# A two-layer hybrid decoder trunk: attention products in split precision, the compressed branch moved to the end of a unit, and the adaLN vectors moved into the FFN blocks

## The chip, the cores and the metric

The kernel runs on one core of one Trainium2 chip. The metric is the device time of the program in microseconds (us), lower is better. All tensors are float32. A product of two float32 tiles is either made directly (F32) or, after a tile has been split into a rounded part (hi, type F32R) and the rest (lo), as three F32R products hi·hi + hi·lo + lo·hi (`mm3`, lines 121 to 124, where the three have a line each).

## The reference

One sequence of 512 positions, width 1024, two layers. Each layer has three sub-layers, each of them modulated by a vector c through shift, scale and gate (adaLN) and closed by a layer norm:

```python
for l in range(DEPTH):
    mod = (silu(c) @ ada_w[l] + ada_b[l]).reshape(Bn, 3, 3, D)   # shift, scale, gate
    x = LN(ALPHA*x + 0.5*(1+gate0) * swiglu(x*(1+scale0)+shift0))
    x = LN(ALPHA*x +     (1+gate1) * mixer (x*(1+scale1)+shift1))
    x = LN(ALPHA*x + 0.5*(1+gate2) * swiglu(x*(1+scale2)+shift2))
```

The mixer is one projection whose columns go to attention, to a gated MLP and to a state-space part, and one output projection over all three. The attention has 8 heads in 2 groups and, for each block of 128 queries, three branches, each with a softmax of its own, weighted with gates and added: compressed keys (31 of them), selected key blocks (all of them here, since the 16 best of 8 are taken), and a window of 512.

## The kernel before

**Order of the work.** Six sub-layers follow each other: FFN, mixer, FFN, FFN, mixer, FFN (n = 0 to 5). An FFN walks over its 22 column blocks in two halves of 11: up products into PSUM, the activation, then the down products. Weights come as 512 KB tiles by DMA from the SP queue, are split by ACT (`hi`) and DVE (`lo`, line 106), and go into `mm3`.

**adaLN vectors.** A vector of 1024 is made by 8 steps of `ada_dot` (line 155): a 512 KB tile of weights is loaded, and DVE multiplies and sums it along its rows with the vector silu(c). `make_bg` hands these steps out: `bg()` is called at fixed places of a sub-layer and issues the next few. The table `share` says how many vectors a sub-layer makes: 4, 3, 3, 3, 3 for n = 0 to 4. Both mixers (n = 1 and n = 4) make three each, beside the attention; `silu_c()` makes silu(c) anew there.

**Attention.** A unit is a pass p (heads 0, 1 or 2, 3 of both groups), a query block qb (3, 2, 1, 0 in this order) and a branch br. There are 24 units in a mixer. `score` makes the scores of four heads (tile S), the softmax numerators (tile P: DVE adds bias and takes the maximum, ACT takes the exponential), and scales them with gate over sum (line 920 on DVE). Two units later `gather` takes the unit in chunks of 128 keys: four transposes on PE (line 938, F32) into a bank of PSUM (`tp`, two banks), a copy to SBUF by ACT (`pt`, line 940), and the product with the values, here called the weigh (line 948): two F32 products, each of which fills one half of the output's partitions (64 value columns) and takes 256 columns of pt. A mixer has 40 chunks in the branches 1 and 2 and 8 in the compressed branch; the two mixers have 80 and 16. All chunks of the three branches of a (p, qb) add up in `op`; after the last, ACT and DVE take it out of PSUM into `hT_hi` and `hT_lo` (lines 958, 959). `op` is a half of the one bank of pool P, so two query blocks share a bank.

**Filler.** Between transposes and weigh, `tick` lets PE go on with a list of jobs: the remaining projections (`pj`), then the part of the output projection that needs no attention (`part`, tile y, closed by `residual`, line 242), and in the second pass `rest`, the part that does. The order of the instructions on every engine is fixed when the program is built, by a scheduler that takes the instruction that it holds to be ready first; on the chip every engine takes them in that order.

Of the kernel before, what the change touches and what calls it, by code (L numbers as in the profile page):

```python
# [11 lines left out]
F32 = mybir.dt.float32  # L12
F32R = mybir.dt.float32r
# [6 lines left out]
T = 512  # L20
# [25 lines left out]
QORDER = (3, 2, 1, 0)  # L46
# [6 lines left out]
def kernel(ctx: ExitStack, tc: tile.TileContext, a: dict, out: bass.AP,  # L53
                             subs=((0, 0), (0, 1), (0, 2), (1, 0), (1, 1), (1, 2))):
    nc = tc.nc
    V, S, G, PE = nc.vector, nc.scalar, nc.gpsimd, nc.tensor
# [14 lines left out]
    def nm(s):  # L71
        count[0] += 1
        return f"{s}_{count[0]}"

    def slab(s, pool="s", dt=F32):
        return sp[pool].tile([128, 512], dt, tag=pool, name=nm(s))

    def big(s):
        return bp.tile([128, 1024], F32, tag="b", name=nm(s))

    def tiny(s, n, dt=F32):
        rot = s in ("mx", "sm", "fc", "st", "mv", "rs", "nr", "gst", "ss")
        return (t4 if rot else t1).tile([128, n], dt, tag=f"t_{s}", name=nm(s))

    def bank(k, s):
        return psp[k].tile([128, 512], F32, tag=k, name=nm(s))
# [34 lines left out]
    def mm3(o, lh, ll, rh, rl, first, last):  # L121
        PE.matmul(o, lh, rh, start=first, stop=False)  # L122
        PE.matmul(o, lh, rl, start=False, stop=False)  # L123
        PE.matmul(o, ll, rh, start=False, stop=last)  # L124
# [17 lines left out]
    def silu_c():  # L142
        csil, c_th = big("csil"), big("cth")
        load(csil, bcast_row(a["c"][0], 1024))
        S.activation(c_th, csil, AF.Tanh, scale=0.5)
        V.scalar_tensor_tensor(csil, c_th, 1.0, csil, op0=ALU.add, op1=ALU.mult)
        cond["c"] = csil
# [43 lines left out]
    def gate_par(l, s, P):  # L191
        g = P["G"] = big("G")
        G.dma_start(g, bcast_row(mods[l, s, 2][0], 1024))
        if s != 1:
            V.tensor_scalar(g, g, 0.25, None, op0=ALU.mult)

    def norm_par(l, s, P):
        P["lg"], P["lb"] = big("lg"), big("lb")
        load(P["lg"], bcast_row(a["ln_g"][l, s], 1024))
        load(P["lb"], bcast_row(a["ln_b"][l, s], 1024))  # L200
# [249 lines left out]
    def mixer(l, P, last, lane, bg, catch_up, gate_params, norm_params):  # L450
# [10 lines left out]
        w2v = p2[:, 256:384]  # L461
        pe = p2[:, 384:416]
        dtb, alog = p2[:, 446:450], p2[:, 450:454]
        dsk, ng = p2[:, 454:456], p2[:, 456:458]
        w3v = wsT.rearrange("p (g t) -> p g t", g=4)
        G.affine_select(w3v, w3v, pattern=[[0, 4], [1, 128]], compare_op=ALU.is_ge, fill=0.0, base=0,
                        channel_multiplier=-1)
# [94 lines left out]
        def pair(t):  # L562
            return [t[:, 0:512], t[:, 512:1024]]
# [250 lines left out]
        V.tensor_sub(kc4[:, :, 1, :], ks4, kc4[:, :, 0, :].bitcast(F32))  # L814
        S.copy(vcm[0:31, :], ps[0:31, 64:192])

        o0 = pair(big("o0"))
        ready = []

# [14 lines left out]
        early = []  # L834
# [93 lines left out]
        def release(n=0):  # L928
            while len(held) > n:
                held.pop(0)()  # L930

        def gather(p, qb, br, pr, op):
            nv = 8 * qb + 7
            for kb in range(1 if br == 0 else qb + 1):
                n = nv if br == 0 else 128
                tp = bank("H", "tp")
                for e in range(4):
                    PE.transpose(tp[0:n, e * 128:(e + 1) * 128], pr[e][:, kb * 128:kb * 128 + n], ident)  # L938
                pt = slab("pt", "q")
                S.copy(pt[0:n, :], tp[0:n, :])  # L940

                def weigh(kb=kb, n=n, pt=pt):
                    for g, r in ((0, lo_half), (1, hi_half)):
                        if br == 0:
                            v = vcm[0:n, g * 64:(g + 1) * 64]
                        else:
                            v = (vS, vW)[br - 1][:, kb * 128 + g * 64:kb * 128 + (g + 1) * 64]
                        PE.matmul(op[r, :], v, pt[0:n, g * 256:(g + 1) * 256], start=(br == 0),  # L948
                                  stop=(br == 2 and kb == qb))
                    if br == 2 and kb == qb:  # L950
                        o3 = op.rearrange("p (i t) -> p i t", i=2)
                        if not ready:
                            early.append(qb)
                            for i in range(2):
                                S.copy(o0[i][:, qb * 128:(qb + 1) * 128], o3[:, i, :])
                            return
                        hh = hT_hi[:, qb, 2 * p:2 * p + 2, :]
                        S.copy(hh, o3)
                        V.tensor_sub(hT_lo[:, qb, 2 * p:2 * p + 2, :], o3, hh.bitcast(F32))

                held.append(weigh)
                tick(TICK_G[p])
                release(HOLD)

        units = [(p, qb, br) for p in range(2) for qb in QORDER for br in range(3)]
        later = {}
        for n, (p, qb, br) in enumerate(units):
            if br == 2 and p == 1:
                later[n + 1] = qb
        def gains(tiles):  # L970
            for k in tiles:
# [50 lines left out]
                    jobs.pop(0)  # L1022
            credit[0] = min(credit[0], 1)

        silu_c()
        probs = [score(*u, TICK_0) for u in units[:LOOK]]
        for n, (p, qb, br) in enumerate(units + [(2, 0, 0)]):
            if n + LOOK < len(units):
                probs.append(score(*units[n + LOOK], TICK_S[n // 12]))
            if n < len(units):  # L1030
                if br == 0:
                    if n % 6 == 0:
                        opt = bank("P", "op")
                    op = opt[:, (n % 6) // 3 * 256:(n % 6) // 3 * 256 + 256]
                gather(p, qb, br, probs[n], op)
            else:
                release()
            bg()
            if n in later:
                jobs.append(rest(later[n]))  # L1040
# [46 lines left out]
    for n, (l, s) in enumerate(subs):  # L1087
        order.append((l, s, 2))
        if n + 1 < len(subs):
            order += [(*subs[n + 1], 1), (*subs[n + 1], 0)]  # L1090
    share = {0: 4, 1: 3, 2: 3, 3: 3, 4: 3}

    def need(*key):
        if key not in mods:
# [49 lines left out]
    for n, (l, s) in enumerate(subs):  # L1144
        last = n == len(subs) - 1
        catch_up = partial(renew, P)
        P = {}

        def params():
            if n:  # L1150
                norm_par(l, s, P)
            if (l, s, 2) in mods:
                gate_par(l, s, P)
            if not last and (*subs[n + 1], 0) in mods:
                next_par(l, s, *subs[n + 1], P)

        if s == 1:
            if not lane:
                for _ in make_bias():
                    pass  # L1160
            need(l, s, 2)
            cond.clear()
            mixer(l, P, last, lane, make_bg(n, P), catch_up, lambda: gate_par(l, s, P), lambda: norm_par(l, s, P))
        else:
            if share.get(n) and "c" not in cond:
                silu_c()
            after_mixer = n > 0 and subs[n - 1][1] == 1
            gated = [None]
            ffn(l, s, P, last, make_bg(n, P, gated), (2, 0) if after_mixer and QORDER[0] == 3 else (0, 2), params,
                catch_up, feed if n == 0 else None, gated)  # L1170
# [90 lines left out]
```

## Time and profile before

| | us |
|---|---|
| median of 3 runs | 2063.02 (2061.39 to 2063.42) |
| the profiled execution, its own time | 2062.94 |
| its span, first to last instruction | 2061.2 |
| PE busy | 2032.4 |
| DVE busy | 1328.4 |
| ACT busy | 764.5 |

The granted clock of PE is full throughout (9 in every slice of the page). A busy PE means that some product is in flight; products overlap, so how fast PE advances is read from the distance between the starts of successive rows of the timeline.

### The profile page before, as it was taken

Reading aid. Unit: us, or ns where it says so; the run is one execution under the profiler, and the core shown is the slowest. Engines: PE = TensorE matmul, PEld = TensorE weight load, DVE = VectorE, ACT = ScalarE, POOL = GpSimd, SP = SyncE. Lnnn points to the kernel's source line nnn. Section 1 sums busy time; section 2 is a strip of 40 time slices with the busy share of each in tenths; the row PEclk is TensorE's granted clock in tenths of the full one; section 3 lists DMA queues with packets and bytes.
Section 4 is the critical chain, followed back from the end, with each engine's and each line's share of the span. In section 5 each row is a group of like instructions: output and inputs, shape, how many; then the busy total and the mean of one; then the engine's idle time right before and its main releaser. Section 6 shows DMA issues by size and latency. Waiting matters only on the chain.

```text
span 2061.2 us, 25919 instructions
## 1 busy us (share of the span) xinstructions
PE 2032.4 (99%) x9992; PEld 1648.3 (80%) x9992; DVE 1328.4 (64%) x2425; ACT 764.5 (37%) x1342; POOL 43.0 (2%) x73
## 2 busy tenths in 40 slices
PE   7999999999999999999999999999999999999998
PEld 6888888987666888888898888889776678888886
DVE  6756438878897647444764644478788975353455
ACT  4422223525657422222442222235256573222221
POOL 0000000000000000000000000000000000000000
PEclk9999999999999999999999999999999999999999
DMA  8755425324452544442444444243254523233221
GB/s 338 259 175 212 153 97 181 106 84 162 138 168 73 193 134 161 135 126 83 161 143 135 151 144 126 88 145 102 92 174 132 169 97 107 79 115 100 93 91 52
DMA packets 85175, 282.34 MB, mean 137 GB/s; under 512 B 13843, under 2 KB 14099, under 8 KB 85052
## 3 DMA queue, kind: packets, MB, share of 16 engines
q1 hardware_dynamic: 82748, 274.88, 40.6%
q0 software_dynamic: 2304, 5.82, 0.8%
q8 instruction: 78, 1.28, 0.3%
q14 instruction: 45, 0.37, 0.1%
HBM read 278.51 MB, written 4.76 MB: 137 GB/s over the span
## 4 chain that ended last, share of the span: by engine, by line
PE 93%; DVE 4%; ACT 1%; DMA 1%; issue 0%; POOL 0%; SPq 0%; DVEq 0%; POOLq 0%; ACTq 0%
PE h L122 15%; PE h L123 15%; PE h L124 15%; PE y L122 9%; PE y L124 9%; PE y L123 9%; PE pj L122 3%; PE pj L124 3%; PE pj L123 3%; PE op L948 2%; PE tp L938 2%; PE S L907 1%; PE S L908 1%; DVE raw L155 1%; PE hps L218 1%; PE hid L641 1%
## 5 line engine op out<-in xcount | busy, mean ns | idle before, releaser
L104 ACT CAST whi<-raw 128x1024 fp32r<-128x1024 f32 x308 | 320.4, 1047 | 747.3 <-issue 393.7
L122 PE MATMUL h<-hT_hi,whi 128*128 128x512 f32 (+1 forms) x1504 | 565.8, 377 | 12.8 <-ACT hT_hi L1081 12.8
L123 PE MATMUL h<-hT_lo,whi 128*128 128x512 f32 (+1 forms) x1504 | 566.4, 377 | 0.0
L124 PE MATMUL h<-hT_hi,wlo 128*128 128x512 f32 (+1 forms) x1504 | 566.1, 376 | 0.0
L106 DVE TENSOR_TENSOR wlo<-raw,whi 128x1024 fp32r<-128x1024 f32 x308 | 372.8, 1216 | 262.0 <-ACT whi L104 261.5
L122 PEld LDWEIGHTS h<-hT_hi,whi 128*128 128x128 f32 x1504 | 283.7, 189 | 63.8 <-ACT hT_hi L1081 12.8
L124 PEld LDWEIGHTS h<-hT_hi,wlo 128*128 128x128 f32 x1504 | 283.9, 189 | 51.5
L123 PEld LDWEIGHTS h<-hT_lo,whi 128*128 128x128 f32 x1504 | 283.9, 189 | 51.5 <-DVE hT_lo L1082 0.4
L124 PE MATMUL y<-whi,glo 128*128 128x512 f32 x576 | 224.2, 389 | 0.0
L122 PE MATMUL y<-whi,ghi 128*128 128x512 f32 x576 | 224.2, 389 | 0.0
L123 PE MATMUL y<-wlo,ghi 128*128 128x512 f32 x576 | 224.2, 389 | 0.0
L333 DVE TENSOR_TENSOR th<-th,h 128x512 f32<-128x512 f32 x88 | 60.4, 687 | 228.6 <-PE h L124 227.9
L155 DVE CUSTOM_DVE_ANT_0 raw<-raw,csil 128x1024 f32<-128x1024 f32 x144 | 174.3, 1218 | 1.6 <-DMA raw<-in_ada_w_dram 1.5
L123 PEld LDWEIGHTS y<-wlo,ghi 128*128 128x128 f32 x576 | 108.2, 188 | 22.5
L124 PEld LDWEIGHTS y<-whi,glo 128*128 128x128 f32 x576 | 108.2, 188 | 22.5
L122 PEld LDWEIGHTS y<-whi,ghi 128*128 128x128 f32 x576 | 108.2, 188 | 22.3
L122 PE MATMUL pj<-hT_hi,whi 128*128 128x512 f32 x288 | 117.4, 408 | 0.0
L123 PE MATMUL pj<-hT_lo,whi 128*128 128x512 f32 x288 | 113.7, 395 | 0.0
L124 PE MATMUL pj<-hT_hi,wlo 128*128 128x512 f32 x288 | 113.4, 394 | 0.0
L102 DVE TENSOR_TENSOR raw<-raw,G 128x1024 f32<-128x1024 f32 x86 | 104.2, 1217 | 2.0 <-DMA raw<-in_w_dram 1.9
L336 ACT CAST ghi<-th 128x512 fp32r<-128x512 f32 x88 | 54.4, 619 | 136.5 <-DVE th L333 136.5
L332 DVE SCALAR_TENSOR_TENSOR th<-th,h 128x512 f32<-128x512 f32 x88 | 60.0, 682 | 38.1 <-ACT th L331 38.1
(285 smaller groups left out, 2516.7 us busy)
## 6 DMA issues: line engine op xcount, KB each, us to landing
raw<-in_w_dram SPq DMA_DIRECT2D x256, 512.0 KB, 3.6
raw<-in_ada_w_dram SPq DMA_DIRECT2D x144, 512.0 KB, 4.4
raw<-in_wS_dram SPq DMA_DIRECT2D x36, 512.0 KB, 3.5
raw<-in_cw_dram SPq DMA_DIRECT2D x16, 512.0 KB, 3.9
raw<-in_wo_dram SPq DMA_DIRECT2D x16, 512.0 KB, 4.5
raw<-in_wl_dram SPq DMA_DIRECT2D x8, 512.0 KB, 9.0
T<-lane SPq DMA_DIRECT2D x16, 256.0 KB, 4.1
lg<-in_ln_g_dram SPq DMA_DIRECT2D x6, 512.0 KB, 5.1
```

The costliest lines, as they stand in the source:

```text
L102: V.tensor_mul(raw, raw, gain)
L104: S.copy(hi[:, :n], raw[:, :n])
L106: V.tensor_sub(lo[:, :n], raw[:, :n], hi[:, :n].bitcast(F32))
L122: PE.matmul(o, lh, rh, start=first, stop=False)
L123: PE.matmul(o, lh, rl, start=False, stop=False)
L124: PE.matmul(o, ll, rh, start=False, stop=last)
L155: V.tensor_tensor_reduce(out=raw, in0=raw, in1=cond["c"], scale=0.5, scalar=0.0, op0=ALU.mult, op1=ALU.add, accum_out=acc[:, k:k + 1])
L332: V.scalar_tensor_tensor(th, th, 1.0, h1, op0=ALU.add, op1=ALU.mult)
L333: freed[0] = V.tensor_mul(th, th, h3).ins
L336: S.copy(hi, th)
L938: PE.transpose(tp[0:n, e * 128:(e + 1) * 128], pr[e][:, kb * 128:kb * 128 + n], ident)
L948: PE.matmul(op[r, :], v, pt[0:n, g * 256:(g + 1) * 256], start=(br == 0), stop=(br == 2 and kb == qb))
```

## The change

The weigh of the branches 1 and 2 becomes an `mm3`: the probabilities are split by ACT (`pt`, now F32R) and DVE (`pl`, a new slab from pool T), the values once for each mixer (`v_hi`, `v_lo`), and each product takes all 128 value columns and all 512 columns of the probabilities. Of its result only the two blocks on the diagonal (a group's values with its own heads) are used. `op` is therefore a whole bank, one for each (p, qb), from a pool that still has one bank. The branches of a (p, qb) come in the order 1, 2, 0, and `settle_heads`, after branch 0, takes each block out of PSUM by itself. The vectors are made in the FFNs alone (`share` 6, 5, 5 for n = 0, 2, 3).

```diff
+        v_hi, v_lo = [pair(bp.tile([128, 1024], F32R, tag="b", name=nm(s_))) for s_ in ("vh", "vl")]
+        for v, h, lo in zip((vS, vW), v_hi, v_lo):
+            S.copy(h, v)
+            V.tensor_sub(lo, v, h.bitcast(F32))
...
+        def settle_heads(p, qb, op):
+            for g, r in ((0, lo_half), (1, hi_half)):
+                o3 = op[r, g * 256:(g + 1) * 256].rearrange("p (i t) -> p i t", i=2)
+                if not ready:
+                    for i in range(2):
+                        S.copy(o0[i][r, qb * 128:(qb + 1) * 128], o3[:, i, :])
+                else:
+                    hh = hT_hi[r, qb, 2 * p:2 * p + 2, :]
+                    S.copy(hh, o3)
+                    V.tensor_sub(hT_lo[r, qb, 2 * p:2 * p + 2, :], o3, hh.bitcast(F32))
...
-                pt = slab("pt", "q")
+                pt = slab("pt", "q", F32 if br == 0 else F32R)
                 S.copy(pt[0:n, :], tp[0:n, :])
-                def weigh(kb=kb, n=n, pt=pt):
+                if br:
+                    pl = slab("pl", "T", F32R)
+                    V.tensor_sub(pl, tp, pt.bitcast(F32))
+                def weigh(kb=kb, n=n, pt=pt, pl=pl if br else None):
+                    if br:
+                        v = slice(kb * 128, (kb + 1) * 128)
+                        mm3(op, v_hi[br - 1][:, v], v_lo[br - 1][:, v], pt, pl, br == 1 and kb == 0, False)
+                        return
                     for g, r in ((0, lo_half), (1, hi_half)):
-                        if br == 0:
-                            v = vcm[0:n, g * 64:(g + 1) * 64]
-                        else:
-                            v = (vS, vW)[br - 1][:, kb * 128 + g * 64:kb * 128 + (g + 1) * 64]
-                        PE.matmul(op[r, :], v, pt[0:n, g * 256:(g + 1) * 256], start=(br == 0),
-                                  stop=(br == 2 and kb == qb))
+                        c = slice(g * 256, (g + 1) * 256)
+                        PE.matmul(op[r, c], vcm[0:n, g * 64:(g + 1) * 64], pt[0:n, c], start=False, stop=True)
+                    settle_heads(p, qb, op)
...
-        units = [(p, qb, br) for p in range(2) for qb in QORDER for br in range(3)]
+        units = [(p, qb, br) for p in range(2) for qb in QORDER for br in (1, 2, 0)]
...
-        silu_c()
...
-                if br == 0:
-                    if n % 6 == 0:
-                        opt = bank("P", "op")
-                    op = opt[:, (n % 6) // 3 * 256:(n % 6) // 3 * 256 + 256]
+                if br == 1:
+                    op = bank("P", "op")
...
-    share = {0: 4, 1: 3, 2: 3, 3: 3, 4: 3}
+    share = {0: 6, 2: 5, 3: 5}
```

Two smaller edits go with it: four columns of a parameter tile are copied to a tile of their own, so that its slab of pool T comes free early (four of its five slabs hold the bias of the pass, tile T, and `pl` takes the fifth), and `next_par` of a mixer moves to where `norm_par` is called.

How the instructions stand: four places in the first mixer. Names carry a buffer's number at the end.

**PE, first query block (qb = 3) of the second pass.** `tp` are transposes, `op` the weighs, `S` scores, `y` filler. Before:

```order
L124 MATMUL y_5102<-whi_4597,hT_lo 128x512
L907 MATMUL S_5154<-kh_3549,qa_4452 128x384
L908 MATMUL S_5154<-kl_3552,qa_4452 128x384
L907 MATMUL S_5160<-kh_3549,qa_4565 128x384
L908 MATMUL S_5160<-kl_3552,qa_4565 128x384
L948 MATMUL op_5055<-pt_5100,vS_2843 64x256 x2
L938 MATMUL tp_5128<-cst,P_4930 128x128
L948 MATMUL op_5055<-pt_5116,vS_2843 64x256 x2
L938 MATMUL tp_5128<-cst,P_4936 128x128
L938 MATMUL tp_5128<-cst,P_4942 128x128
L938 MATMUL tp_5128<-cst,P_4948 128x128
```

With the change:

```order
L122 MATMUL op_5149<-pt_5155,vh_3944 128x512
L123 MATMUL op_5149<-pl_5157,vh_3944 128x512
L124 MATMUL op_5149<-pt_5155,vl_3945 128x512
L122 MATMUL op_5149<-pt_5167,vh_3944 128x512
L123 MATMUL op_5149<-pl_5169,vh_3944 128x512
L124 MATMUL op_5149<-pt_5167,vl_3945 128x512
L122 MATMUL op_5149<-pt_5179,vh_3944 128x512
L957 MATMUL tp_5186<-cst,P_5035 128x128
L957 MATMUL tp_5186<-cst,P_5041 128x128
L957 MATMUL tp_5186<-cst,P_5047 128x128
L957 MATMUL tp_5186<-cst,P_5053 128x128
L123 MATMUL op_5149<-pl_5181,vh_3944 128x512
```

Before, a weigh stood behind filler or transposes of another chunk and needed `pt` alone. Now the second product of a weigh needs `pl`, in two of the three weighs shown it stands right behind the first, and no y stands among them.

**PE, between two query blocks of the second pass.** The weigh of the compressed branch closes the block (`op_5000`), the next block has the next bank (`op_5149`). With the change:

```order
L971 MATMUL op_5000<-pt_5123,vcm_3940 64x256 x2
L957 MATMUL tp_5150<-cst,P_5053 128x128
L957 MATMUL tp_5162<-cst,P_5035 128x128
L957 MATMUL tp_5162<-cst,P_5041 128x128
L957 MATMUL tp_5162<-cst,P_5047 128x128
L957 MATMUL tp_5162<-cst,P_5053 128x128
L957 MATMUL tp_5174<-cst,P_5035 128x128
L957 MATMUL tp_5174<-cst,P_5041 128x128
L957 MATMUL tp_5174<-cst,P_5047 128x128
L957 MATMUL tp_5174<-cst,P_5053 128x128
L122 MATMUL op_5149<-pt_5155,vh_3944 128x512
```

Nine transposes stand between the last product into the old bank and the first into the new one; before, the two blocks of a pair had halves of one bank and no such place stood between them.

**DVE, at the same place.** `hT_lo<-op` are the two instructions that take the old bank's low part out, `pl` the split, P the scaling of the block's second branch. Before (the end of the first block of the pass), and with the change:

```order
L155 ISA raw_5223,mod_912_5071<-raw_5223,csil_3888 128x1024
L155 ISA mod_912_5071 128x1
L889 TENSOR_TENSOR Pc_5082<-Pc_5082,sm_5086 128x4x23
L863 TENSOR_SCALAR sm_5153<-sm_5153 128x4
L959 TENSOR_TENSOR hT_lo<-op_5055,hT_hi 128x256
L864 RECIPROCAL sm_5153<-sm_5153 128x4
L910 ISA P_5229,mx_5226<-S_5228,T_4878 128x384
L910 ISA mx_5226 128x1
L867 TENSOR_TENSOR sm_5153<-sm_5153,gts_2842 128x4
```

```order
L947 TENSOR_TENSOR hT_lo<-op_5000,hT_hi 64x256
L873 TENSOR_TENSOR sm_5086<-sm_5086,gts_2900 128x4
L962 TENSOR_TENSOR pl_5157<-tp_5150,pt_5155 128x512
L926 TENSOR_SCALAR P_5088<-P_5088,sm_5086 128x512
L926 TENSOR_SCALAR P_5094<-P_5094,sm_5086 128x512
L926 TENSOR_SCALAR P_5100<-P_5100,sm_5086 128x512
L926 TENSOR_SCALAR P_5106<-P_5106,sm_5086 128x512
L947 TENSOR_TENSOR hT_lo<-op_5000,hT_hi 64x256
L962 TENSOR_TENSOR pl_5169<-tp_5162,pt_5167 128x512
```

Before, one instruction took the result out, with an adaLN step (line 155) two rows ahead of it; now there are two, and a split and four scalings stand between them.

**DVE, where the second pass starts.** The last residual of `part` (x_sb<-x_sb,y) stood behind the first scores of the pass, with two more to come; before:

```order
L910 ISA P_4942,mx_4927<-S_4941,T_4884 128x512
L910 ISA mx_4927 128x1
L863 TENSOR_SCALAR sm_4899<-sm_4899 128x4
L910 ISA P_4948,mx_4927<-S_4947,T_4887 128x512
L910 ISA mx_4927 128x1
L864 RECIPROCAL sm_4899<-sm_4899 128x4
L242 SCALAR_TENSOR_TENSOR x_sb<-x_sb,y_4915 128x512
```

With the change, the last of the eight residuals stands ahead of the first score of the pass:

```order
L962 TENSOR_TENSOR pl_5008<-tp_5001,pt_5006 128x512
L106 TENSOR_TENSOR wlo_4914<-raw_4909,whi_4912 128x1024
L106 TENSOR_TENSOR wlo_4921<-raw_4916,whi_4919 128x1024
L947 TENSOR_TENSOR hT_lo<-op_4787,hT_hi 64x256
L886 TENSOR_TENSOR Pc_4986<-Pc_4986,Sc_4981 128x4x7
L242 SCALAR_TENSOR_TENSOR x_sb<-x_sb,y_5010 128x512
L888 TENSOR_REDUCE mx_4989<-Pc_4986 128x4
L916 ISA P_5035,mx_5032<-S_5034,T_5020 128x512
L916 ISA mx_5032 128x1
```

So the filler that these residuals close has moved into the first pass.

## Rows read from the trace of the kernel before

**Rows 1.** The page: span, engines, and the chain that ended last by engine.

```profile
span 2061.2 us, 25919 instructions
PE 2032.4 (99%) x9992; PEld 1648.3 (80%) x9992; DVE 1328.4 (64%) x2425; ACT 764.5 (37%) x1342; POOL 43.0 (2%) x73
...
PE 93%; DVE 4%; ACT 1%; DMA 1%; issue 0%; POOL 0%; SPq 0%; DVEq 0%; POOLq 0%; ACTq 0%
```

**Rows 2.** Windows, passes of mixer 1: length; PE, PEld, DVE, ACT, POOL busy; clock, DMA, GB/s.

```profile
505.50:593.06 87.56, 86.58 (x486) 61.02 (x483) 79.56 (x230) 51.31 (x128) 1.66 (x1) 1.00 0.48 146
593.06:655.40 62.34, 61.65 (x357) 42.11 (x356) 53.57 (x203) 42.34 (x112) 3.29 (x6) 1.00 0.37 119
```

**Rows 3.** The timeline of PE in the first pass (start us, us, engine, line).

```profile
516.30 0.39 PE L124 MATMUL pj<-hT_hi,wlo 128*128 128x512 f32 x1
516.61 0.65 PE L948 MATMUL op<-pt,vS 128*64 128x256 f32 x4
517.20 0.50 PE L122 MATMUL pj<-hT_hi,whi 128*128 128x512 f32 x1
517.53 0.39 PE L123 MATMUL pj<-hT_lo,whi 128*128 128x512 f32 x1
517.76 0.40 PE L124 MATMUL pj<-hT_hi,wlo 128*128 128x512 f32 x1
...
518.45 0.40 PE L124 MATMUL pj<-hT_hi,wlo 128*128 128x512 f32 x1
518.78 0.65 PE L948 MATMUL op<-pt,vS 128*64 128x256 f32 x4
519.36 0.66 PE L938 MATMUL tp<-cst,P 128*128 128x128 f32 x4
519.78 0.48 PE L122 MATMUL pj<-hT_hi,whi 128*128 128x512 f32 x1
520.10 0.39 PE L123 MATMUL pj<-hT_lo,whi 128*128 128x512 f32 x1
```

**Rows 4.** Groups of instructions, shapes apart (count, busy us, mean ns).

```profile
L940 ACT COPY pt<-tp 128x512 f32<-128x512 f32 x80 | 45.7, 584 | 62.9 <-PE tp L938 61.9
L247 DVE TENSOR_TENSOR x_sb<-y,x_sb 128x512 f32<-128x512 f32 x42 | 28.8, 686 | 16.5 <-PE y L124 16.2
L959 DVE TENSOR_TENSOR hT_lo<-op,hT_hi 128x256 fp32r<-128x256 f32 x14 | 5.9, 420 | 4.1 <-ACT hT_hi L958 4.1
L155 DVE CUSTOM_DVE_ANT_0 raw<-raw,csil 128x1024 f32<-128x1024 f32 x144 | 174.3, 1218 | 1.6 <-DMA raw<-in_ada_w_dram 1.5
L155 DVE DVE_READ_ACCUMULATOR2_ANT mod<- 128x1 f32 x128 | 10.5, 82 | 0.0
L920 DVE TENSOR_SCALAR P<-P,sm 128x512 f32<-128x512 f32 x28 | 11.8, 482 | 0.0
```

**Rows 5.** Waits of PE over the whole span (us in total, times, longest).

```profile
PE op L948 <- ACT pt L940: 2.6, 5, 0.8
```

**Rows 6.** Tile op, 588 to 660 us: what its engine idled for, us, times.

```profile
  ACT pt L940: 4.8, 15
```

**Rows 7.** The timeline where op changes banks in the second pass, all engines.

```profile
636.23 0.65 PE L948 MATMUL op<-pt,vW 128*64 128x256 f32 x2
636.80 0.50 PE L122 MATMUL y<-whi,hT_hi 128*128 128x512 f32 x1
636.91 0.37 ACT L958 CAST hT_hi<-op 128x256 fp32r<-128x256 f32 x1 [1.38 <-PE op L948]
637.92 0.42 DVE L959 TENSOR_TENSOR hT_lo<-op,hT_hi 128x256 fp32r<-128x256 f32 x1
641.03 0.43 PE L948 MATMUL op<-pt,vcm 15*64 15x256 f32 x2
```

**Rows 8.** Windows, end of the first FFN half; columns as in rows 2.

```profile
140.00:160.00 20.00, 20.00 (x90) 16.58 (x89) 20.00 (x27) 4.51 (x5) 0.00 (x0) 1.00 0.87 302
160.00:180.00 20.00, 20.00 (x90) 16.57 (x89) 17.21 (x22) 5.25 (x5) 0.00 (x0) 1.00 0.84 298
```

More of the change, by code (lines that the diff above doesn't have):

```diff
@@ L463, in mixer @@
         dtb, alog = p2[:, 446:450], p2[:, 450:454]
-        dsk, ng = p2[:, 454:456], p2[:, 456:458]
+        skn = tiny("skn", 4)
+        V.tensor_copy(skn, p2[:, 454:458])
+        dsk, ng = skn[:, 0:2], skn[:, 2:4]
         w3v = wsT.rearrange("p (g t) -> p g t", g=4)
@@ L930, in release @@
                 held.pop(0)()
+        def settle_heads(p, qb, op):
[8 more added lines that the diff above has]
+                    V.tensor_sub(hT_lo[r, qb, 2 * p:2 * p + 2, :], o3, hh.bitcast(F32))
+            if not ready:
+                early.append(qb)
         def gather(p, qb, br, pr, op):
@@ L938, in gather @@
                     PE.transpose(tp[0:n, e * 128:(e + 1) * 128], pr[e][:, kb * 128:kb * 128 + n], ident)
-                pt = slab("pt", "q")
+                pt = slab("pt", "q", F32 if br == 0 else F32R)
                 S.copy(pt[0:n, :], tp[0:n, :])
-                def weigh(kb=kb, n=n, pt=pt):
-                    for g, r in ((0, lo_half), (1, hi_half)):
-                        if br == 0:
-                            v = vcm[0:n, g * 64:(g + 1) * 64]
-                        else:
-                            v = (vS, vW)[br - 1][:, kb * 128 + g * 64:kb * 128 + (g + 1) * 64]
-                        PE.matmul(op[r, :], v, pt[0:n, g * 256:(g + 1) * 256], start=(br == 0),
-                                  stop=(br == 2 and kb == qb))
[L950 to L959, printed above, removed]
+                if br:
[6 more added lines that the diff above has]
+                        return
+                    for g, r in ((0, lo_half), (1, hi_half)):
+                        c = slice(g * 256, (g + 1) * 256)
+                        PE.matmul(op[r, c], vcm[0:n, g * 64:(g + 1) * 64], pt[0:n, c], start=False, stop=True)
+                    settle_heads(p, qb, op)
                 held.append(weigh)
@@ L963, in gather @@
                 release(HOLD)
-        units = [(p, qb, br) for p in range(2) for qb in QORDER for br in range(3)]
+        units = [(p, qb, br) for p in range(2) for qb in QORDER for br in (1, 2, 0)]
         later = {}
         for n, (p, qb, br) in enumerate(units):
-            if br == 2 and p == 1:
+            if br == 0 and p == 1:
                 later[n + 1] = qb
@@ L1162, with last_params @@
             cond.clear()
-            mixer(l, P, last, lane, make_bg(n, P), catch_up, lambda: gate_par(l, s, P), lambda: norm_par(l, s, P))
+            def last_params():
+                norm_par(l, s, P)
+                next_par(l, s, *subs[n + 1], P)
+            mixer(l, P, last, lane, make_bg(n, P), catch_up, lambda: gate_par(l, s, P), last_params)
         else:
```

## The prediction

> **What bounds the kernel now.** I read the page first, then the two passes of a mixer's attention as windows, then the timeline around one weigh, then the waits, and last the FFN stretch in which DVE is fullest. On the page PE is busy for 2032.4 of 2061.2 us and holds 93% of the chain that ended last [rows 1]: time goes down only if PE has less to do or waits less. In both passes of the attention PE is busy but for 1.0 and 0.7 us, and DVE, which feeds it, for 91% and 86% of the time [rows 2]. So there is hardly a wait to take away, but a feeder that is nearly full. Over the whole span PE waits for a copy of transposed probabilities five times, 2.6 us in all [rows 5]; its weight loads, which run ahead, waited for one 15 times in the second pass alone [rows 6]. In that pass a weigh mostly starts when its `pt` arrives, with little to spare.
>
> **The profiled execution** took 2062.94 us, 1.7 us more than its span of 2061.2 [rows 1], and is 0.1 us from the median, 2063.02. The sum is made against 2062.9. About 0.2% of it, 4 us, is what a measurement can tell from no change.
>
> **The change, part by part.**
>
> *The weigh on PE.* Successive F32R products of 512 columns start 0.23 us apart (517.53 to 517.76) [rows 3]. A weigh put between two such products moves the second one's successor from 2 x 0.23 = 0.46 to 1.23 us (516.30 to 517.53): it costs 0.77, of which 0.58 is its own (516.61 to 517.20), 0.08 is lost in going into it and 0.10 in coming out [rows 3]. Three F32R products cost 3 x 0.23 = 0.69, with nothing lost on either side: 0.08 less. Where transposes follow, weigh and transposes cost 1.65 - 0.46 = 1.19 (518.45 to 520.10); afterwards 0.69 + 0.42 for the transposes + 0.09 for coming out of them = 1.20 [rows 3]: nothing gained. In the order of before, 46 of 96 weighs stand ahead of an F32R product and 50 ahead of an F32 one. For the 80 weighs that change this makes 38 x -0.08 + 42 x 0.01 = **-2.7 us**. Bounds: -6.4 if all 80 are of the first kind; 0 if the roughly 30 places where the new order puts transposes straight ahead of one of the products lose 0.09 each.
>
> The premise, that the whole array is worth more than its halves, is what the rows deny: the four records of a weigh take 0.58 us together, where the two shown by themselves take 0.43 [rows 3, 7], so the halves work side by side already. The Trainium skill, TensorEngine Tiling (Array Packing), section Key Properties, says the same and speaks against this change: tiles of the array run matmuls in parallel, and only changing the mode drains it. By that rule the saving is the 0.08 and 0.10 at the edges, which the trace has; if the halves took turns, a weigh would take 1.16 and the change save some 80 x 0.58 = 46 us.
>
> *The wait for `pl`.* No row shows this split. Its nearest is a DVE subtraction of 128x512 that reads PSUM, 0.69 us; the cast ahead of it is the copy of now, 0.58 [rows 4]. From the end of the last transpose's step (0.10 each [rows 3]) the chain is some 0.17 until its data is out, 0.58 cast, 0.69 split and three hand-offs of 0.03 (636.88 to 636.91 [rows 7]): 1.5 to 1.6 us, with ACT and DVE free. I counted what the new order lets PE do between a chunk's last transpose and the product with `pl`, at 0.23 for 512 columns and 0.10 for a transpose: 3.1 us on average over a mixer's 40 chunks, but under 1.57 in 6 places, short by 1.4 us in all. A DVE that is 90% full does not answer at once: the subtraction at 637.92 came 0.64 after its cast was done at 637.28 [rows 7]. With that added the chain is 2.2 us and PE has less in 17 of 40, short by 9.8 in all. Bounds 1.4 and 9.8 a mixer. I take the middle, **5.6 a mixer**: the row with 0.64 is of this very kind, but the steps of 1.22 us that fill DVE there are gone. Pool T leaves `pl` a single slab, so a split also waits for the product before it; that belongs to the upper bound.
>
> *The bank.* `op` has one bank, and now every query block needs it empty. At the start of the second pass the order lists, after the last product into it: cast 0.37 [rows 7], its subtraction 0.42, one split 0.69, four scalings at 0.48, the second subtraction 0.42, in all 0.37 + 0.42 + 0.69 + 1.93 + 0.42 = 3.8 us [rows 4]; PE has nine transposes, 0.95 us, so 2.9 wait. At the next block the scalings are of 384 columns (about 0.42 each by that row's size) and PE has 2.1 us: 1.5. At the third PE has some 5 us of filler: 0. That is 4.4, **say 4.3 a mixer**. Bounds: 0, as now, when bank changes had 4.15 us of other work beside 2.1 us of emptying (636.88 to 641.03 [rows 7]); 6.3 with 0.64 more at each.
>
> *The filler.* The order moves the filler of `part` ahead of the second pass. It makes no work, but takes the cover from that pass, which has the short places above; with cover gone everywhere, see the last rival.
>
> *The end.* After the last weigh one cast (0.37) and one subtraction (0.42) more stand ahead of the final products: **0.8 a mixer**, bounds 0 and 0.8.
>
> *DVE in a mixer.* Out go 24 steps at 1.218 + 0.082 = 31.2 us and the making of silu(c); in come 40 splits of 0.69, 7 subtractions of 0.42 and two of 0.69 for the values: 27.4 + 2.9 + 1.4 = 31.7 [rows 4]. DVE is as full as before; what it does is more urgent. The values' splits stand beside projections on PE and count nothing; without that cover 2.5 us.
>
> *The FFNs.* Three of them get 16 steps each, 20.8 us of DVE. PE keeps its pace in the fullest stretch (90 products in each 20 us) with DVE busy for 37.2 of 40 us [rows 8]. In the first FFN the rate goes from 38 to 56 steps in 29 calls; 11 calls in a half's down product make 8.9 us more. Splits of weights run several tiles ahead, so I count 0; if that lead is used up, 8.9 less the 2.8 idle us, 6. The 48 loads that leave the mixers' SP queue join the weights' on the FFNs'; DMA is 1% of the chain [rows 1], so 0.
>
> *Old waits.* The 2.6 us for `pt` fall into the new wait for `pl`: **-2.6**, bounds -2.6 and 0.
>
> **Sum:** 2 x (5.6 + 4.3 + 0.8) - 2.7 - 2.6 = +16.1, from 2062.9 to **2079 us**. By the bounds the same case runs from 2060 to 2097.
>
> **The rivals.**
> 1. *Faster.* The scheduler's order holds on the chip: each `pl` is there before the first product's 0.23 us are over, banks are emptied behind filler as at 636 us [rows 7], and the switches at the edges of the weighs are saved everywhere. Price -6.4 - 2.6: 2054. For it: an average cover of 3.1 us against a chain of 1.6. Against it: 17 short places, and products split up by transposes. It decides at the DVE queue: below some 0.2 us ahead of `pl` it holds.
> 2. *No difference.* As before, but the short places cost their 1.4 a mixer and the products gain only 2.7: 2063.
> 3. *The FFN pays.* The weighs come out even and the first FFN's late weight splits cost 6 us: 2069. Against it: PE shows no slip in a stretch with 93% DVE [rows 8].
> 4. *The second pass is bound by the chain.* Without filler, each of its 20 chunks pays cast and split anew, about 1.3 us: 26 a mixer, 2115. Against it: two `tp` banks let two chunks overlap.
>
> **How the numbers follow.** Forecast 0.52, rivals 0.16, 0.18, 0.06, 0.08. Faster: 0.16 (rival 1). Same: 0.18 (rival 2). Slower: 0.52 + 0.06 + 0.08 = 0.66. The range 2055 to 2100 leaves out about half of rival 1, rival 4, and a little of the forecast's top.
>
> **What would show it.** Right: PE waits for `pl`, 17 or so times a mixer and mostly in the second pass; a wait of one to three us at the second and third bank of that pass; the second pass longer than 62.3 us; FFNs unchanged. Wrong: windows of both passes shorter together than 149.9 us; or products of `op` without a wait; or FFN windows with fewer than 89 products in 20 us, which would be rival 3. If weighs of three products took other than 0.69 us, the first term would be wrong.

## The result, and the profile after

The changed kernel takes 2088.67 us (median of 4 runs, 2087.63 to 2089.67) against 2062.99 for the kernel before: 1.0127 of it, 95% interval 1.0115 to 1.0139, or +25.7 us. The forecast was 2079 with a range of 2055 to 2100: the sign and the range hold, and the forecast's own range of 2060 to 2097 too, but the loss is 1.6 times the predicted 16.1. The profiled execution took 2087.63 us, 1.0 below the median. From its page, to set beside [rows 1]:

```profile
span 2085.9 us, 25874 instructions
PE 2046.5 (98%) x9912; PEld 1682.1 (81%) x9912; DVE 1393.5 (67%) x2524; ACT 775.6 (37%) x1363; POOL 42.5 (2%) x73
...
PE 93%; DVE 3%; ACT 2%; DMA 1%; issue 1%; SPq 0%; POOL 0%; DVEq 0%; ACTq 0%; POOLq 0%
```

The span grew by 24.7 us, PE's busy time by 14.1: the rest is waiting. Where it went is read from the first product of each stage in PE's timelines (hps of line 218 opens a mixer, h the FFN behind it):

| stage | before | after | |
|---|---|---|---|
| to mixer 1 | 365.31 | 365.67 | +0.4 |
| mixer 1 | 304.35 | 316.03 | +11.7 |
| the two FFNs between | 715.70 | 715.79 | +0.1 |
| mixer 2 | 304.55 | 317.06 | +12.5 |
| last FFN, to the end of the span | 371.29 | 371.35 | +0.1 |

Nearly all of it stands in the mixers. The windows from the first score of a mixer to the first of its second pass, and from there to the last weigh; first mixer 1 before (length; PE, PEld, DVE, ACT, POOL busy; clock, DMA, GB/s):

```profile
503.73:593.06 89.33, 88.35 (x500) 62.31 (x500) 81.25 (x235) 52.78 (x131) 1.66 (x1) 1.00 0.49 148
593.06:660.53 67.47, 66.78 (x383) 45.01 (x381) 56.73 (x213) 44.61 (x117) 3.29 (x6) 1.00 0.34 110
```

The same after, both mixers:

```profile
502.14:597.09 94.95, 94.21 (x504) 74.60 (x503) 82.21 (x225) 54.39 (x131) 1.66 (x1) 1.00 0.15 50
597.09:672.13 75.04, 69.15 (x352) 50.88 (x350) 62.72 (x217) 48.20 (x127) 1.11 (x2) 0.95 0.15 50
1533.50:1628.45 94.95, 94.21 (x503) 74.61 (x502) 82.18 (x225) 54.44 (x131) 1.66 (x1) 1.00 0.16 50
1628.45:1704.96 76.51, 70.89 (x352) 52.03 (x350) 62.89 (x217) 48.49 (x127) 1.11 (x2) 0.93 0.14 49
```

In the first pass PE idles for 0.7 us (1.0 before). In the second it idles for 5.9 and 5.6 us in place of 0.7, and there its granted clock is no longer 1.00. The first pass is longer by 5.6 us, about what its additional filler takes: the windows of tile y alone, before and, below, after (PE, PEld, DVE busy and counts):

```profile
503.73:593.06 89.33, 18.08 (x66) 11.68 (x66) 3.39 (x5) 1.00 0.49 148
593.06:660.53 67.47, 31.26 (x101) 17.78 (x101) 5.41 (x8) 1.00 0.34 110
```

```profile
502.14:597.09 94.95, 24.18 (x90) 16.08 (x90) 4.78 (x7) 1.00 0.15 50
597.09:672.13 75.04, 23.64 (x78) 13.56 (x77) 4.09 (x6) 0.95 0.15 50
```

24 products of the filler have left the second pass for the first, 5.5 us at 0.23 [rows 3]. (The kernel with nothing but the vectors moved, share_only in the next section, has 66 and 96 in the same windows; the 5 that its second pass lacks stand behind the last weigh.) By the code, not by a run, that is the new order of branches: `score` calls `tick` for each of four heads in the branches 1 and 2 and never in the compressed one, and the two units scored ahead at line 1038 are now both of the former kind. Four jobs more are handed out at the start, of six products each.

Where the second pass starts, PE's timeline after (start us, us, engine, line; in brackets the idle time and what ended it):

```profile
608.53 0.34 PE L914 MATMUL S<-kl,qa 128*128 128x384 f32 x1
609.25 0.33 PE L957 MATMUL tp<-cst,P 128*128 128x128 f32 x1 [0.39 <-ACT P L924]
609.85 0.72 PE L957 MATMUL tp<-cst,P 128*128 128x128 f32 x2 [0.27 <-DVE P L926]
610.51 0.65 PE L971 MATMUL op<-pt,vcm 7*64 7x256 f32 x4
611.09 0.77 PE L957 MATMUL tp<-cst,P 128*128 128x128 f32 x5
612.91 1.12 PE L957 MATMUL tp<-cst,P 128*128 128x128 f32 x4 [1.06 <-DVE pl L962]
614.95 0.79 PE L122 MATMUL op<-pt,vh 128*128 128x512 f32 x1 [0.92 <-DVE hT_lo L947]
615.54 0.63 PE L123 MATMUL op<-pl,vh 128*128 128x512 f32 x1
615.97 0.63 PE L124 MATMUL op<-pt,vl 128*128 128x512 f32 x1
616.40 0.63 PE L122 MATMUL op<-pt,vh 128*128 128x512 f32 x1
```

And DVE's at the same place:

```profile
610.58 1.22 DVE L106 TENSOR_TENSOR wlo<-raw,whi 128x1024 fp32r<-128x1024 f32 x1
611.71 0.17 DVE L870 RECIPROCAL sm<-sm 128x4 f32<-128x4 f32 x1
611.80 0.39 DVE L947 TENSOR_TENSOR hT_lo<-op,hT_hi 64x256 fp32r<-64x256 f32 x1
612.11 0.15 DVE L873 TENSOR_TENSOR sm<-sm,gts 128x4 f32<-128x4 f32 x1
612.18 0.68 DVE L962 TENSOR_TENSOR pl<-tp,pt 128x512 fp32r<-128x512 f32 x1
612.78 1.66 DVE L926 TENSOR_SCALAR P<-P,sm 128x512 f32<-128x512 f32 x4
614.47 0.43 DVE L947 TENSOR_TENSOR hT_lo<-op,hT_hi 64x256 fp32r<-64x256 f32 x1
```

This is the row of DVE work that the forecast listed: subtraction, split, four scalings, subtraction. PE has no y product to go on with; four transposes wait 1.06 us for a `tp` bank that the split still reads, and the first product into the new bank waits 0.92 for the second subtraction. Then the products of op start 0.43 us apart, not 0.23: the clock has fallen, as the windows there show (the granted clock is the third number from the right):

```profile
608.00:612.00 4.00, 3.12 (x16) 1.43 (x14) 4.00 (x11) 3.16 (x9) 0.00 (x0) 1.00 0.39 96
612.00:616.00 4.00, 2.16 (x7) 1.58 (x8) 2.87 (x8) 1.48 (x4) 0.00 (x0) 0.51 0.51 166
616.00:620.00 4.00, 4.00 (x15) 2.64 (x13) 2.31 (x6) 0.59 (x1) 0.00 (x0) 0.63 0.02 6
620.00:624.00 4.00, 3.96 (x22) 3.08 (x22) 3.73 (x14) 2.98 (x9) 0.00 (x0) 1.00 0.00 0
```

Where PE does not wait, the three products of a weigh start 0.23 us apart, as the forecast has it; of the rows below, the first had its weight load (PEld) late, and the next one follows 0.33 us later:

```profile
600.57 0.50 PE L122 MATMUL op<-pt,vh 128*128 128x512 f32 x1
600.90 0.40 PE L123 MATMUL op<-pl,vh 128*128 128x512 f32 x1
601.14 0.39 PE L124 MATMUL op<-pt,vl 128*128 128x512 f32 x1
```

Waits of PE over the span after (us, times, longest), beside [rows 5]:

```profile
PE y L122 <- ACT hT_hi L946: 5.2, 6, 1.4
...
PE tp L957 <- ACT P L924: 2.0, 4, 0.6
PE op L122 <- DVE hT_lo L947: 1.8, 2, 0.9
PE tp L957 <- DVE pl L962: 1.6, 2, 1.1
```

**A ledger of both mixers, in us,** from the distances between the starts of successive rows of PE:

| | mixer 1 | mixer 2 | both | forecast |
|---|---|---|---|---|
| PE idle (2.6 to 8.2 and 3.2 to 7.5), and three products of op that stood late with no idle time marked | +6.4 | +5.2 | +11.6 | +18.8 |
| products and transposes at the lower clock, beyond their time at the higher | +3.2 | +5.2 | +8.4 | 0 |
| the weighs of branches 1 and 2 | +1.2 | +1.5 | +2.7 | -2.7 |
| the rest (compressed weighs and small groups) | +0.9 | +0.6 | +1.5 | 0 |
| sum | +11.7 | +12.5 | +24.2 | +16.1 |

Each line is good to about 0.3. The second one counts what the products took beyond their time at the higher clock; what the lower clock cost the kernel is less, since some of it replaces waits (see P_S). The third line, mixer 1: 120 products at their unrounded distance of 0.2275 take 27.3 against 24.6 for the weighs before (+2.7), 29 of the products lose 0.11 behind an F32 row or a late weight load (+3.2), and y, pj and Sc lose 4.7 less, since fewer weighs stand among them.

### The profile page after: what moved, and what is told of

It reads as the page before. It is cut to its first block, busy times and chain, and to the rows that moved or that the text cites. A ratio compares the mean times of both kernels' runs of the same rounds, so it can differ in the third digit from the quotient of the medians.

```text
span 2085.9 us, 25874 instructions
## 1 busy us (share of the span) xinstructions
PE 2046.5 (98%) x9912; PEld 1682.1 (81%) x9912; DVE 1393.5 (67%) x2524; ACT 775.6 (37%) x1363; POOL 42.5 (2%) x73
## 4 chain that ended last, share of the span: by engine, by line
PE 93%; DVE 3%; ACT 2%; DMA 1%; issue 1%; SPq 0%; POOL 0%; DVEq 0%; ACTq 0%; POOLq 0%
PE h L122 15%; PE h L124 15%; PE h L123 15%; PE y L122 9%; PE y L124 9%; PE y L123 9%; PE pj L122 3%; PE pj L124 3%; PE pj L123 3%; PE tp L957 1%; PE op L123 1%; PE op L122 1%; PE S L913 1%; PE op L124 1%; PE hps L218 1%; PE S L914 1%
## 5 line engine op out<-in xcount | busy, mean ns | idle before, releaser
L918 ACT ACTIVATE P<-P,mx 128x512 f32<-128x512 f32 (+3 forms) x128 | 70.9, 556 | 30.8 <-DVE mx L916 30.8
```

The costliest lines, as they stand in the source:

```text
L918: S.activation(w, w, AF.Exp, bias=m, scale=-1.0, accum_out=sm[:, e:e + 1])
```

## The experiments

Each kernel was timed beside the kernel before (2062 to 2063 us); the number in brackets is the ratio to it with its interval. What is to be told apart: the forecast's theory, that the split's chain and the one bank make PE wait in the attention, against the moved vectors, the single slab, and the moved filler.

**share_only: the kernel before with the vectors moved and nothing else.**

```diff
-    share = {0: 4, 1: 3, 2: 3, 3: 3, 4: 3}
+    share = {0: 6, 2: 5, 3: 5}
```

The `silu_c()` of the mixers and the place of `next_par` go with the table, here and, the other way round, in old_share.

> The kernel before with nothing changed but the table of vectors (6, 5, 5 in the FFNs, none in a mixer). If the attention's new weigh costs all of it, as the forecast has it, this stays within 4 us of the kernel before: 2058 to 2065, the mixers shorter by up to 2 us each since DVE has 31 us less in them, the FFNs longer by less than 1 us together. If instead the moved vectors set the loss (they let the filler of the attention run early, and the second pass is left bare), this is slower by 5 us or more: 2068 to 2085.

Measured 2060.95 (ratio 0.9990, 0.9981 to 1.0000). The moved vectors cost nothing in the FFNs and give about 1.6 us. The rest of the change (the split, the branch order and the bank together) thus costs 27.7 us beside them, not 25.7.

**old_share: the changed kernel with the table of before.**

```diff
-    share = {0: 6, 2: 5, 3: 5}
+    share = {0: 4, 1: 3, 2: 3, 3: 3, 4: 3}
```

> The changed kernel with the table of before (4, 3, 3, 3, 3): both the new weigh and the 24 steps of 1.22 us stand in a mixer. If DVE's load beside the split decides, it is slower than the changed kernel by 10 to 30 us: 2098 to 2120. If the moved vectors are what hurts, it comes back to 2065 to 2078.

Measured 2116.45 (1.0255, 1.0238 to 1.0272), 27.8 above the changed kernel. The second pass of mixer 1, in the same columns:

```profile
598.72:687.72 89.00, 75.59 (x353) 54.85 (x351) 78.00 (x256) 48.13 (x126) 3.24 (x6) 0.88 0.37 125
```

PE idles for 13.4 us there, and the first pass has 2.4 idle where the changed kernel has 0.7. The longest waits there are for what DVE or the emptying of the bank delivers (3.7 us for pl, 3.6 for hT_hi, 2.2 for hT_lo). So DVE's load beside the split counts, and moving the vectors out is what keeps the change from costing twice as much.

**no_pl: no low part of the probabilities.**

```diff
-                    V.tensor_sub(pl, tp, pt.bitcast(F32))
...
-                        mm3(op, v_hi[br - 1][:, v], v_lo[br - 1][:, v], pt, pl, br == 1 and kb == 0, False)
+                        PE.matmul(op, v_hi[br - 1][:, v], pt, start=br == 1 and kb == 0, stop=False)
+                        PE.matmul(op, v_lo[br - 1][:, v], pt, start=False, stop=False)
```

> The changed kernel without the low part of the probabilities: the split on DVE and the second of the three products of a weigh are left out, so a part of the products is not computed. The 80 products take 18 us with them by 0.23 each. If the waits for pl cost 5.6 us a mixer, as the forecast has it, 11 more go: 2059. If emptying the bank and the clock that falls there cost the loss, and pl little, only the 18 go: 2070, and the low clock in the second pass stays. If without the split the bank's wait goes as well, 2052.

Measured 2058.18 (0.9982, 0.9973 to 0.9991): 30.5 less than the changed kernel, 18.2 of it the 80 products and 12.3 waits and clock. Mixer 1:

```profile
502.08:592.73 90.65, 89.82 (x486) 71.42 (x485) 71.22 (x207) 54.37 (x135) 1.66 (x1) 1.00 0.19 64
592.73:656.49 63.76, 60.10 (x331) 45.66 (x329) 50.53 (x195) 47.81 (x123) 1.11 (x2) 1.00 0.13 42
```

The first pass falls by 4.3 us, about its 20 products (4.6): there the split was covered. The second falls by 11.3, 6.7 more than its products; in mixer 2 it falls from 76.51 to 65.00. The 12.3 is a mixture: the clock still fell (mean 0.97 in the second pass of mixer 2), and the ten executions go from 2056.0 to 2062.1, the four at a mean granted clock of 0.997 3.9 us above the four at 0.999.

**pl_s: pl from the pool of 16 slabs.**

```diff
-                    pl = slab("pl", "T", F32R)
+                    pl = slab("pl", "s", F32R)
```

> The changed kernel with pl taken from the pool of 16 slabs (s) in place of the one free slab of pool T. In the changed kernel DVE waited 2.9 us a mixer for that slab. If the single slab matters to PE, 2 to 4 us a mixer go: 2081 to 2085. If DVE's queue and the chain cast-split set the time at which pl is there, nothing goes: 2087 to 2090.

Measured 2087.31 (1.0119, 1.0104 to 1.0134), 1.4 under the changed kernel, which is within what can be told. The single slab, which the forecast put into its upper bound, is not what costs.

**t08: filler given back to the second pass.**

```diff
-TICK_G = (1, 1)
+TICK_G = (0.8, 1)
```

> The changed kernel with 0.8 in place of 1 filler job for each chunk of the first pass, so that 113 filler products (y) stand in the second pass in place of 77, and 54 in place of 90 in the first. The loss stands in the second pass. If it is the cover that is missing there, the waits and the low clock in it shrink by about half and the first pass stays as it is: 2072 to 2080. If the split's chain and DVE set the pace in both passes, the loss only changes its place: 2085 to 2092.

Measured 2082.9 (1.0097, 1.0082 to 1.0112): 5.8 gained, less than half of the loss; between the two expectations. Mixer 1:

```profile
501.64:590.79 89.15, 87.35 (x470) 68.57 (x469) 79.57 (x230) 54.23 (x133) 1.67 (x1) 1.00 0.19 65
590.79:670.36 79.57, 76.16 (x385) 57.67 (x383) 63.82 (x213) 48.49 (x124) 1.12 (x2) 0.96 0.11 34
```

The second pass, with 36 products (8.2 us) more, idles for 3.4 in place of 5.9, but now the first one, with 36 fewer (54, and so fewer than the 66 of before), idles for 1.8 in place of 0.7.

**P_S: the bank of op by turns from two pools.**

```diff
-                    op = bank("P", "op")
+                    op = bank("P" if qb % 2 else "S", "op")
```

> The changed kernel with the banks of op taken by turns from pool P and from the pool of the scores (S, three banks), so that a new query block need not wait until the old one's bank is emptied. If the bank is what starts the waits and the low clock at the first bank change of the second pass (about 5 us a mixer with the clock), 2077 to 2081 and no low clock at that place. If the splits set the pace there, or the scores miss their bank as much, 2085 to 2092.

Measured 2083.18 (1.0104, 1.0087 to 1.0120): 5.5 gained, short of the first expectation. The second passes of its two mixers:

```profile
597.04:668.93 71.89, 66.22 (x350) 49.01 (x349) 62.27 (x217) 48.19 (x127) 1.12 (x2) 1.00 0.15 52
...
1625.84:1700.12 74.28, 70.06 (x350) 51.86 (x349) 62.58 (x217) 47.99 (x127) 1.12 (x2) 0.93 0.15 50
```

The same work twice, with one difference: in mixer 1 the clock stayed up, in mixer 2 it did not. That costs 2.4 us net. By the Trainium skill, TensorE: Matmul & The Clock Gate, section Terms, the penalty is the throttled time times the share of the clock that is held back, here 0.07 x 74.28 = 5.2 as an estimate. The net is under half of the rule's: the row of mixer 2 idles for 1.5 us less, so a slower PE also waits less. The four executions of P_S show little of it too: between mean granted clocks of 0.998 and 0.994 lie 0.004 of the time, 8.3 us, but it goes from 2083.05 to 2084.56 only. In no_pl nearly all of it shows: 0.002, 4.1 us, and 3.9 measured.

**rest_later: the last products of a block one unit later.**

```diff
-                later[n + 1] = qb
+                later[min(n + 2, 24)] = qb
```

> The changed kernel with the last part of the output projection (rest) released one unit later, two units after a block's compressed branch in place of one. PE waits 2.6 us a mixer for hT_hi ahead of such a product. If that wait is a loss of its own, 5 us go: 2083 to 2085. If the products only fill a place in which PE would wait for a split anyway, it stays or gets worse: 2087 to 2094.

Measured 2084.14 (1.0107, 1.0092 to 1.0122): 4.5 gained, in the range of the first expectation; the wait of y for hT_hi fell from 5.2 to 2.7 us. So that wait is at least in part a loss of its own. But new waits for pl came up (1.3 us), and the intervals of this kernel and the changed one overlap.

**act_empties: ACT alone takes op out of its bank**, into a slab `ho` from which hT_hi and hT_lo are made.

```diff
-                    S.copy(hh, o3)
-                    V.tensor_sub(hT_lo[r, qb, 2 * p:2 * p + 2, :], o3, hh.bitcast(F32))
+                    S.copy(f3, o3)
+            if ready:
+                S.copy(hh, f3)
+                V.tensor_sub(hT_lo[:, qb, 2 * p:2 * p + 2, :], f3, hh.bitcast(F32))
```

> The changed kernel with the bank of op emptied by ACT alone: two copies into a slab, from which one cast and one subtraction make hT_hi and hT_lo, off the path to the next block. If DVE's two subtractions, with a split and four scalings between them, hold the bank, 1.5 to 2.5 us a mixer go at each first bank change: 2082 to 2086. If the wait passes to pt and pl, which stand behind the same engines, 2087 to 2091.

Measured 2081.2 (1.0090, 1.0075 to 1.0105): 7.5 gained, more than the first expectation, since in mixer 1 the clock stayed up as well:

```profile
597.57:669.11 71.54, 66.38 (x351) 48.86 (x349) 60.50 (x213) 49.27 (x130) 1.12 (x2) 1.00 0.15 52
```

PE still idles for 5.2 us, 0.7 less than in the changed kernel, while the pass is 3.5 shorter: the wait passes to pt and pl (over the span 3.8 and 2.0 us for op), and most of the gain is the clock.

**half_split: splits in the first pass only**; the second has the weighs, branch order and bank of before.

```diff
-                if br:
+                split = br and p == 0
+                if split:
...
-        units = [(p, qb, br) for p in range(2) for qb in QORDER for br in (1, 2, 0)]
+        units = [(p, qb, br) for p in range(2) for qb in QORDER for br in ((0, 1, 2) if p else (1, 2, 0))]
```

> The changed kernel with the split weighs in the first pass alone; the second pass has the weighs, the order of branches and the bank of the kernel before. If the whole loss stands in the second pass (the first one is longer by its own filler only), this is even with the kernel before and with the one that has nothing but the vectors moved: 2058 to 2064. If the splits cost as much in the first pass, half of the loss stays: 2072 to 2078.

Measured 2081.45 (1.0090, 1.0075 to 1.0105). Both expectations miss. Mixer 1:

```profile
501.40:598.74 97.34, 96.60 (x518) 76.60 (x517) 83.80 (x227) 56.09 (x133) 1.66 (x1) 1.00 0.17 50
598.74:668.16 69.42, 64.93 (x353) 40.66 (x351) 48.91 (x192) 44.99 (x122) 1.12 (x2) 0.95 0.14 53
```

The first pass, which has the splits, idles for 0.7; the second, which has none, for 4.5, and the clock falls there. It has 66 filler products; share_only, with the same weighs, has 96. So the theory that the loss stands where the split weighs stand falls. A new one: it stands where filler is missing. One thing is particular to this kernel: where its passes meet, two compressed branches follow each other, an order that neither the kernel before nor the changed one has. 2.8 of the 4.5 us are scores that wait for DVE at 605 to 614 us, soon behind that place.

**half_split_85 and filler_early: the two halves of that theory apart.** The first has the splits of half_split with the filler of share_only (66 and 96 products); the second has no split and the filler of half_split (96 and 66).

```diff
-TICK_G = (1, 1)
+TICK_G = (0.85, 1)
```

> Splits in the first pass alone, as in half_split, with 0.85 filler jobs for each chunk of the first pass: 66 filler products stand in the first pass and 96 in the second, as in the kernel with the vectors moved alone (half_split had 96 and 66). If the place of the filler is what half_split paid for, 2058 to 2064. If the first pass's splits themselves hand their lateness on to the second pass, 2074 to 2082.

```diff
-TICK_G = (1, 1)
+TICK_G = (1.2, 1)
```

> The kernel with the vectors moved alone and no split at all (2061 us), with 1.2 filler jobs for each chunk of the first pass: 96 filler products in the first pass and 66 in the second, as in half_split. If the second pass needs its filler as cover, whatever its weighs are, this is slower by 8 to 20 us: 2069 to 2081. If only a kernel with splits needs it, 2060 to 2064.

Measured 2070.76 (1.0039, 1.0027 to 1.0052) and 2064.41 (1.0008, 0.9999 to 1.0017), so both expectations of half_split_85 miss, and filler_early lies 0.4 us above its second. The two causes work together:

| filler products in the passes | no split | splits in the first pass |
|---|---|---|
| 66 and 96 | 2060.95 | 2070.76 |
| 96 and 66 | 2064.41 | 2081.45 |

Early filler costs 3.5 us without a split and 10.7 with it; the split costs 9.8 with late filler and 17.0 with early. "Split" is here the whole of the change in the first pass, branch order and bank with it, and the place where the passes meet. Mixer 1 of half_split_85:

```profile
502.05:597.80 95.75, 93.02 (x501) 73.22 (x501) 82.12 (x233) 55.01 (x137) 1.66 (x1) 0.98 0.19 62
597.80:664.24 66.44, 66.15 (x379) 44.34 (x377) 49.72 (x187) 45.13 (x117) 1.12 (x2) 1.00 0.12 41
```

With the filler back in the second pass that one is whole (0.3 idle, full clock), and now the first pass idles for 2.7 us with its clock at 0.98: the waits went where the filler is short.

**relief: t08, P_S, rest_later and act_empties together** (their four edits).

> The changed kernel with four remedies at once: bank emptied by ACT alone, the bank taken by turns from two pools, rest one unit later, and 0.8 filler jobs for each chunk of the first pass. Alone they gave 7, 5.5, 4.5 and 6 us. If they are losses apart, 2066 to 2070. If they are one loss, the first bank changes of the second pass with the low clock behind them, the sum is that of the best two at most: 2074 to 2080, and what is left is the wait for pl.

Measured 2072.24 (1.0045, 1.0029 to 1.0062): 16.4 gained, where the four alone sum to 23.3. So the four are neither losses apart nor a single one. It stays 11.3 above share_only. No split version beat the kernel before; share_only is the fastest that computes all, by 0.1%, at the edge of what can be told.

## Why the prediction came out right in sign and short in size

- **The weigh on PE, forecast -2.7:** the products do start 0.23 apart (600.90, 601.14, 601.37 after), and the edges did leave the other products. But they did not go: some 56 products of op in the two mixers now lose about 0.1 themselves. A little under half of them stand behind an F32 row: these are the forecast's roughly 30 places at 0.09, which made its upper bound 0. The others stand behind F32R rows, most of them with a weight load that waited for pl, pt or the bank. Measured +2.7, beyond that bound: the term had the transposes right and lacked the late loads, which the profile shows as no idle time of PE.
- **The wait for pl, forecast 5.6 a mixer:** the split priced by its nearest row was exact (0.69, though that row, line 247, is an addition; the split's median after is 0.69, the cast's 0.59). Weight loads waited for it 12 times a mixer (7.1 us in both), not 17, and PE itself is listed as idle for it for 1.6 us in both. Taking the split out gives 12.3 us of waits and clock by the medians. That this is near the 11.2 forecast is no proof of the term, since it holds the clock, which the forecast left out, and waits for the bank that the splits prolong. In the first pass, with 24 more products of filler, the split is covered.
- **The bank, forecast 4.3 a mixer:** place and order on DVE were right. The first change shows waits of 1.06 (for a `tp` bank that a split holds) and 0.92 us where 2.9 was listed. At the second, priced at 1.5, no product of op is marked as waiting; the y ahead of it waits 1.35 for hT_hi. act_empties and P_S give 3.7 and 2.7 a mixer, a good part of it the clock that did not fall in mixer 1. The wait of y for hT_hi, 2.6 a mixer, hangs on the same emptying; of it the text had only the end, 0.8, and the stretch from the last weigh to the next FFN grew by 0.4 (9.13 to 9.57).
- **The old waits, forecast -2.6:** PE's waits of op for `pt` are gone from the list. But they are 0.7 in share_only as well: the freed DVE takes most of them away.
- **DVE as full as before, the FFNs 0:** held. DVE is busy for 82.2 us in the first pass against 81.3, the FFNs between the mixers take 715.8 us against 715.7, and the windows of [rows 8] now hold 89 products in place of 90. Rival 3 is out, by the stages and by share_only.
- **The filler, forecast 0:** the prediction says that it "makes no work, but takes the cover", and gives that no price of its own; it left it to rival 4, at 26 a mixer for a second pass bound by the chain. Moved beside splits in one pass it cost 10.7 us over both mixers, and 3.5 without splits; in the changed kernel, giving 36 products back gained 5.8. So the loss of cover was named, but it should have stood in the sum, and rival 4 had it at 52 for both mixers, twice the whole loss. What it costs in the changed kernel alone is not known, since half_split differs from it where the passes meet.
- **The clock, not in the sum:** it fell at the waits of the second passes. By the ledger 8.4 us were lost to the lower clock, the largest thing that the forecast lacked. Part of them replace a wait, as in P_S (2.4 us net in one pass), so 8.4 is rather the upper end of what the clock cost.
- **Its arithmetic:** 38 x -0.08 + 42 x 0.01 is -2.6, not -2.7, and the bank's parts sum to 4.4, not 4.3. The low end of 2060 takes the weighs at -2.7; with their own bound of -6.4 it is 2057. The 2.1 us of emptying at 636 us count the weigh in; from its end, 636.88, to the end of the subtraction it is 1.5. None of this changes the forecast by more than 0.2 us.

The waits, which the sum was made of, are smaller in the ledger than forecast (11.6 against 18.8); the loss is larger because the weighs gave nothing back and the clock fell. So the forecast had the kind of loss right, a second pass in which PE waits for pl and for the bank, and that the sum came within 8.1 us of the ledger's 24.2 is in part luck: 7.2 too much for waits stands against 5.4 too little for weighs, 8.4 for the clock and 1.5 for the rest. Of its signs, the longer second pass (75.0 us) and the unchanged FFNs came; the wait at the second and third bank came at the first change alone, just under a microsecond. What stays open: the shares of the 27.7 us beside share_only do not add up one by one, since remedies overlap, and a fall of the clock comes and goes with them. The changed kernel with as much filler in each pass as before (66 and 101) was not run, nor one with more filler in both. Nor was the new order of branches run with the handing out of jobs at the start as before: that the counter explains the 24 products is read from the code and from their number alone. How splits in the first pass make the second one wait, as in half_split, is not shown either.

## What to carry to other kernels

Filler is a sum to be spent: here some 160 products cover the chains of both passes, and a chain that is 0.69 us longer for each chunk was free in the pass that had gained cover (no_pl) and not in the one that had lost it. An edit that reorders units can move it through a counter that no line of the diff shows, so count the filler of each stage before and after. A wait that leaves PE idle may cost its clock too; here the products behind it then started 0.43 us apart in place of 0.23.

## What the runs showed that was not expected

The granted clock fell to half (1.2 GHz) in the middle of the kernel, in both mixers: at about 612 us, with PE idle for 0.39 and 0.27 us ahead of it, 1.06 across it and 0.92 behind it, and back at about 619; at about 1643 for some 10 us. It does not follow from the order of instructions alone: in P_S and act_empties it stayed up in mixer 1 and fell in mixer 2. In half_split_85 it fell in the first pass, in the second of two waits; the two products behind it take 2.08 us, where they take 1.02 in the kernel before:

```profile
552.32 0.38 PE L913 MATMUL S<-kh,qa 128*128 128x256 f32 x1 [0.77 <-DVE Pc L886]
552.54 0.28 PE L914 MATMUL S<-kl,qa 128*128 128x256 f32 x1
554.23 2.08 PE L793 MATMUL rbc<-dg,cst 128*128 128x512 f32 x2 [1.41 <-DVE dg L790]
```

So in these runs waits and the lower clock came together where the cover was short, in either pass.
